# A row softmax on one core: the unrolled stream replaced by hardware loops of three turns over five slots, with placed loop heads and the last tile on its own

## The chip, the cores and the metric

The kernel runs on one core of one Trainium2 chip. The metric is the device time of one execution in microseconds (us), median over several executions.

Engines: DVE is VectorE, ACT is ScalarE, SP is SyncE, which here only issues loads. Sixteen DMA engines move the data.

## The reference

```python
def reference(x, temperature):            # x: (32, 512, 1024) float32, temperature 0.5
    scaled = x / temperature
    shifted = scaled - np.max(scaled, axis=-1, keepdims=True)
    exp_x = np.exp(shifted)
    return (exp_x / np.sum(exp_x, axis=-1, keepdims=True)).astype(np.float32)
```

There are 16,384 rows of 1,024 numbers: 67.11 MB are read and 67.11 MB are written.

## The kernel before

A tile is 1,024 rows: 128 partitions with 8 rows of 4 KiB each, so 32 KiB per partition and 4 MiB per tile. There are 16 tiles and six buffers. SP issues the loads, ACT the stores. A tile is worked on in two groups of four rows. The order is pipelined by one group: the maximum and the exponentials of group g come before the division of group g-1, so a tile's last division waits behind the first maximum of the next tile.

```python
TILES = [[8]] * 16
BUFS = 6
GROUP = 4
# ... (helpers cut)
    def maximum(g):       # DVE: tensor_reduce over 128x4x1024, then bias = -scale * top
    def exponential(g):   # ACT: four activations Exp(scale*x + bias), in place, with accum_out
    def divide(g):        # DVE: reciprocal of the sums, then four in-place multiplies
    def store(g):
        i, _, _, part = groups[g]
        if part:
            a, k = part
            nc.scalar.dma_start(out=dram(of, i)[:, a : a + k, :], in_=tiles[i][:, a : a + k, :])
            if a + k == sum(TILES[i]):
                load()            # the next tile, when its buffer is free

    with tc.manual_schedule():
        for _ in range(BUFS):
            load()
        for g in range(len(groups) + 1):
            if g < len(groups):
                maximum(g)
                exponential(g)
            if g > 0:
                divide(g - 1)
                store(g - 1)
```

Of the kernel before, what the change touches and what calls it, by code (L numbers as in the profile page):

```python
# [1 line left out]

# [4 lines left out]



TILES = [[8]] * 16  # L10
BUFS = 6

GROUP = 4


@with_exitstack
def kernel(
    ctx: ExitStack,
    tc: tile.TileContext,
    x: bass.AP,  # L20
    temperature: bass.AP,
    out: bass.AP,
):
    nc = tc.nc
    f32 = mybir.dt.float32
    scale = 1.0 / float(temperature)
    extreme = mybir.AluOpType.max if scale > 0 else mybir.AluOpType.min

    P = 128
    xf = x.flatten_outer_dims()  # L30
    of = out.flatten_outer_dims()
    n, d = xf.shape
    assert sum(sum(ks) for ks in TILES) * P == n

    data = ctx.enter_context(tc.tile_pool(name="data", bufs=BUFS))
    stats = ctx.enter_context(tc.tile_pool(name="stats", bufs=4))


    groups, first, r = [], [], 0
    for i, ks in enumerate(TILES):  # L40
        first.append(r)
        r += sum(ks)
        a = 0
        for k in ks:
            for b in range(0, k, GROUP):
                m = min(GROUP, k - b)
                groups.append((i, a + b, m, (a, k) if b + m == k else None))
            a += k

    def dram(t, i):  # L50
        k = sum(TILES[i])
        block = t[P * first[i] : P * (first[i] + k), :]
        return block.rearrange("(p k) d -> p k d", p=P, k=k)

    tiles, small = [], []

    def load():
        i = len(tiles)
        if i < len(TILES):
            xt = data.tile([P, sum(TILES[i]), d], f32, name="xt")  # L60
            nc.sync.dma_start(out=xt, in_=dram(xf, i))  # L61
            tiles.append(xt)

    def maximum(g):
        i, a, k, _ = groups[g]
        top, bias, sums, recip = (
            stats.tile([P, k], f32, name=name) for name in ("top", "bias", "sums", "recip")
        )
        small.append((bias, sums, recip))
        nc.vector.tensor_reduce(  # L70
            out=top, in_=tiles[i][:, a : a + k, :], axis=mybir.AxisListType.X, op=extreme
        )
        nc.vector.tensor_scalar_mul(bias, in0=top, scalar1=-scale)  # L73

    def exponential(g):
        i, a, k, _ = groups[g]
        bias, sums, _ = small[g]
        for b in range(k):
            nc.scalar.activation(  # L79
                tiles[i][:, a + b, :],  # L80
                tiles[i][:, a + b, :],
                mybir.ActivationFunctionType.Exp,
                bias=bias[:, b : b + 1],
                scale=scale,
                accum_out=sums[:, b : b + 1],
            )

    def divide(g):
        i, a, k, _ = groups[g]
        _, sums, recip = small[g]  # L90
        nc.vector.reciprocal(recip, sums)  # L91
        for b in range(k):
            nc.vector.tensor_scalar_mul(  # L93
                tiles[i][:, a + b, :], in0=tiles[i][:, a + b, :], scalar1=recip[:, b : b + 1]
            )

    def store(g):
        i, _, _, part = groups[g]
        if part:
            a, k = part  # L100
            nc.scalar.dma_start(out=dram(of, i)[:, a : a + k, :], in_=tiles[i][:, a : a + k, :])
            if a + k == sum(TILES[i]):
                load()



    with tc.manual_schedule():
        for _ in range(BUFS):
            load()
        for g in range(len(groups) + 1):  # L110
            if g < len(groups):
                maximum(g)
                exponential(g)
            if g > 0:
                divide(g - 1)
                store(g - 1)


# [1 line left out]
_INS = ['x', 'temperature']  # L120
_OUTS = [((32, 512, 1024), 'float32')]

_NUMBERS = {'temperature': 0.5}


# [26 lines left out]
```

## Time and profile before

| | before |
|---|---|
| time, median (3 runs at first; 6 runs with the change) | 318.15 us; 318.08 us |
| span of the profiled run | 316.0 us |
| DMA, whole span | 134.25 MB, 425 GB/s |
| DVE busy, ACT busy | 235.5 us (75%), 149.6 us (47%) |
| interval between tiles in the middle (first maximum to first maximum) | 19.35 us |

The page of the kernel before has two rows for the DMA engines over 40 slices of the span (busy tenths, then GB/s), and a part with the queues: q1 are the loads, q10 the stores, q14 the packets that the page calls instruction (below they are read as fetches of instructions).

```profile
DMA  8999999999999999999999999999999999999996
GB/s 332 411 452 423 373 460 415 452 425 431 436 427 440 427 444 423 444 419 448 415 452 411 452 408 456 423 444 427 436 431 432 440 423 444 419 444 419 452 411 274
...
q1 hardware_dynamic: 2304, 67.11, 49.7%
q10 hardware_dynamic: 2304, 67.11, 49.2%
q14 instruction: 4, 0.03, 0.0%
```

The DMA engines are full from start to end. The next view gives stretches of the span of the kernel before; the last two columns are the mean share of the 16 DMA engines that was busy, and GB/s.

```profile
core 0: us, DVE busy (x) ACT busy (x) POOL busy (x), PEclk, DMA share, GB/s
...
100.00:200.00 100.00, 76.31 (x76) 48.84 (x85) 0.00 (x0) 1.00 1.01 435
200.00:280.00 80.00, 59.22 (x57) 39.28 (x68) 0.00 (x0) 1.00 1.00 433
...
310.00:312.00 2.00, 0.00 (x0) 0.00 (x0) 0.00 (x0) 1.00 0.95 410
312.00:314.00 2.00, 0.00 (x0) 0.00 (x0) 0.00 (x0) 1.00 0.42 180
314.00:316.00 2.00, 0.00 (x0) 0.00 (x0) 0.00 (x0) 1.00 0.00 0
```

The middle runs at 433 to 435 GB/s with a busy share of 1.00 to 1.01.

The timeline of DVE in the kernel before, steady part (start, duration, engine, line, operation). In brackets is the idle time before the instruction and what ended it:

```profile
243.90 4.42 DVE L70 TENSOR_REDUCE top<-xt 128x4 f32<-128x4096 f32 x1 [4.88 <-DMA xt<-in_x_dram]
...
251.29 4.41 DVE L70 TENSOR_REDUCE top<-xt 128x4 f32<-128x4096 f32 x1
...
256.02 2.74 DVE L93 TENSOR_SCALAR xt<-xt,recip 128x1024 f32<-128x1024 f32 x4
263.25 4.42 DVE L70 TENSOR_REDUCE top<-xt 128x4 f32<-128x4096 f32 x1 [4.49 <-DMA xt<-in_x_dram]
```

A tile costs DVE about 14.8 us; then it waits 4.5 us for the next load. DVE does not bound the kernel.

### The profile page before, as it was taken

Reading aid. Unit: us, or ns where it says so; the run is one execution under the profiler, and the core shown is the slowest. Engines: PE = TensorE matmul, PEld = TensorE weight load, DVE = VectorE, ACT = ScalarE, POOL = GpSimd, SP = SyncE. Lnnn points to the kernel's source line nnn. Section 1 sums busy time; section 2 is a strip of 40 time slices with the busy share of each in tenths; the row PEclk is TensorE's granted clock in tenths of the full one; section 3 lists DMA queues with packets and bytes.
Section 4 is the critical chain, followed back from the end, with each engine's and each line's share of the span. In section 5 each row is a group of like instructions: output and inputs, shape, how many; then the busy total and the mean of one; then the engine's idle time right before and its main releaser. Section 6 shows DMA issues by size and latency. Waiting matters only on the chain.

```text
span 316.0 us, 620 instructions
## 1 busy us (share of the span) xinstructions
DVE 235.5 (75%) x224; ACT 149.6 (47%) x257; POOL 0.2 (0%) x4
## 2 busy tenths in 40 slices
DVE  0399999999689494994949859497693976949720
ACT  0176666666526255361554605546064560645500
POOL 0000000000000000000000000000000000000000
DMA  8999999999999999999999999999999999999996
GB/s 332 411 452 423 373 460 415 452 425 431 436 427 440 427 444 423 444 419 448 415 452 411 452 408 456 423 444 427 436 431 432 440 423 444 419 444 419 452 411 274
DMA packets 4612, 134.25 MB, mean 425 GB/s; under 512 B 512, under 2 KB 512, under 8 KB 512
## 3 DMA queue, kind: packets, MB, share of 16 engines
q1 hardware_dynamic: 2304, 67.11, 49.7%
q10 hardware_dynamic: 2304, 67.11, 49.2%
q14 instruction: 4, 0.03, 0.0%
HBM read 67.11 MB, written 67.11 MB: 425 GB/s over the span
## 4 chain that ended last, share of the span: by engine, by line
DVE 49%; DMA 32%; another core or an unknown queue 9%; ACT 5%; issue 1%; DVEq 0%; SPq 0%
DVE top L70 29%; DMA xt<-in_x_dram 20%; DVE xt L93 18%; DMA out_dram<-xt 12%; ACT xt L79 5%; DVE recip L91 1%; DVE bias L73 1%; DVEq L147 0%; SPq L61 0%
## 5 line engine op out<-in xcount | busy, mean ns | idle before, releaser
L79 ACT ACTIVATE xt<-xt,bias 128x1024 f32<-128x1024 f32 x128 | 145.4, 1137 | 136.8 <-DVE recip L91 119.4
L70 DVE TENSOR_REDUCE top<-xt 128x4 f32<-128x4096 f32 x32 | 141.3, 4416 | 62.6 <-DMA xt<-in_x_dram 62.6
L93 DVE TENSOR_SCALAR xt<-xt,recip 128x1024 f32<-128x1024 f32 x128 | 87.7, 749 | 1.1
L79 ACT ACTIVATION_READ_ACCUMULATOR xt<-xt,bias 128x1 f32 x128 | 23.9, 187 | 0.0
L79 ACT ACT_TABLE_LOAD x1 | 1.3, 1283 | 13.0 <-DMA xt<-in_x_dram 13.0
L91 DVE RECIPROCAL recip<-sums 128x4 f32<-128x4 f32 x32 | 5.5, 171 | 2.1 <-ACT xt L79 2.1
L73 DVE TENSOR_SCALAR bias<-top 128x4 f32<-128x4 f32 x32 | 5.4, 170 | 1.1
L133 POOL MEMSET const-bfloat16-1.0<- 128x1 bf16 x1 | 0.1, 101 | 0.0
L133 POOL MEMSET const-uint8-127<- 128x1 uint8 x1 | 0.1, 101 | 0.0
L133 POOL MEMSET const-float32-0.0<- 128x1 f32 x1 | 0.1, 98 | 0.2 <-issue 0.2
L133 POOL MEMSET const-float32-1.0<- 128x1 f32 x1 | 0.1, 98 | 0.0
## 6 DMA issues: line engine op xcount, KB each, us to landing
xt<-in_x_dram SPq DMA_DIRECT2D x16, 4096.0 KB, 50.2
out_dram<-xt ACTq DMA_DIRECT2D x16, 4096.0 KB, 38.6
```

What stands on the lines that cost most here:

```text
L70: nc.vector.tensor_reduce(out=top, in_=tiles[i][:, a : a + k, :], axis=mybir.AxisListType.X, op=extreme)
L73: nc.vector.tensor_scalar_mul(bias, in0=top, scalar1=-scale)
L79: nc.scalar.activation(tiles[i][:, a + b, :], tiles[i][:, a + b, :], mybir.ActivationFunctionType.Exp, bias=bias[:, b : b + 1], scale=scal ...
L91: nc.vector.reciprocal(recip, sums)
L93: nc.vector.tensor_scalar_mul(tiles[i][:, a + b, :], in0=tiles[i][:, a + b, :], scalar1=recip[:, b : b + 1])
L133: nc = _bacc.Bacc("TRN2", target_bir_lowering=False, num_devices=1)
```

## The change

The intent is a much shorter program. DVE and ACT run a hardware loop of three turns over five slots of 32 KiB per partition; the sixteenth tile follows the loop and leaves in two halves. Semaphores are handled by hand. Each loop's head is placed by the argument `head_slot` (66); the program has padding ahead of the head and jumps over it. A tile is now finished before the next is begun.

```diff
-TILES = [[8]] * 16
-BUFS = 6
+SLOTS = 5
+ROWS = 8
+LAST = [4, 4]
 GROUP = 4
+HEAD = 66
# ... (most helpers cut)
+    def take(engine, sem, count=1):
+        engine.wait_ge(sem, count).then_inc(sem, -count)
+    def tile_on_vector(s, ends):
+        take(nc.vector, loaded[s], 16)
+        for a in starts:
+            maximum(s, a)
+        for a in starts:
+            divide(s, a, ends)
+    with tc.tile_critical():
+        for t in range(turns):
+            for s in range(SLOTS):
+                if t > 0:
+                    nc.sync.wait_ge(stored[s], 16 * t)
+                nc.sync.dma_start(...).then_inc(loaded[s], 16)
+        nc.sync.wait_ge(stored[0], 16 * turns)
+        nc.sync.dma_start(out=ring[:, 0], in_=last_tile(xf)).then_inc(loaded[0], 16)
+        with nc.vector.bass.Fori(0, turns, engines=[nc.vector.engine], head_slot={nc.vector.engine: HEAD}):
+            for s in range(SLOTS):
+                tile_on_vector(s, [ROWS])
+        tile_on_vector(0, ends)
+        # ... (one warm-up activation)
+        with nc.scalar.bass.Fori(0, turns, engines=[nc.scalar.engine], head_slot={nc.scalar.engine: HEAD}) as t:
+            for s in range(SLOTS):
+                for a in starts:
+                    exponential(s, a)
+                take(nc.scalar, scaled)
+                nc.scalar.dma_start(out=by_turn(of)[s][:, bass.ds(t, 1), :], ...).then_inc(stored[s], 16)
+        for a in starts:
+            exponential(0, a)
+        for k, b, sem in zip(LAST, ends, finished):
+            take(nc.scalar, scaled)
+            nc.scalar.dma_start(out=last_tile(of)[:, b - k : b, :], ...).then_inc(sem, 16)
# ... (final waits cut)
```

More of the change, by code (lines that the diff above doesn't have):

```diff
@@ L32 @@
     n, d = xf.shape
-    assert sum(sum(ks) for ks in TILES) * P == n
-    data = ctx.enter_context(tc.tile_pool(name="data", bufs=BUFS))
-    stats = ctx.enter_context(tc.tile_pool(name="stats", bufs=4))
-    groups, first, r = [], [], 0
-    for i, ks in enumerate(TILES):
-        first.append(r)
-        r += sum(ks)
-        a = 0
-        for k in ks:
-            for b in range(0, k, GROUP):
-                m = min(GROUP, k - b)
-                groups.append((i, a + b, m, (a, k) if b + m == k else None))
-            a += k
@@ L50, in dram @@
-    def dram(t, i):
-        k = sum(TILES[i])
-        block = t[P * first[i] : P * (first[i] + k), :]
-        return block.rearrange("(p k) d -> p k d", p=P, k=k)
-    tiles, small = [], []
-    def load():
-        i = len(tiles)
-        if i < len(TILES):
-            xt = data.tile([P, sum(TILES[i]), d], f32, name="xt")
-            nc.sync.dma_start(out=xt, in_=dram(xf, i))
-            tiles.append(xt)
-    def maximum(g):
-        i, a, k, _ = groups[g]
-        top, bias, sums, recip = (
-            stats.tile([P, k], f32, name=name) for name in ("top", "bias", "sums", "recip")
-        )
-        small.append((bias, sums, recip))
-        nc.vector.tensor_reduce(
-            out=top, in_=tiles[i][:, a : a + k, :], axis=mybir.AxisListType.X, op=extreme
-        )
-        nc.vector.tensor_scalar_mul(bias, in0=top, scalar1=-scale)
@@ L75, in exponential @@
-    def exponential(g):
-        i, a, k, _ = groups[g]
-        bias, sums, _ = small[g]
-        for b in range(k):
-            nc.scalar.activation(
-                tiles[i][:, a + b, :],
-                tiles[i][:, a + b, :],
-                mybir.ActivationFunctionType.Exp,
-                bias=bias[:, b : b + 1],
-                scale=scale,
-                accum_out=sums[:, b : b + 1],
-            )
-    def divide(g):
-        i, a, k, _ = groups[g]
-        _, sums, recip = small[g]
-        nc.vector.reciprocal(recip, sums)
-        for b in range(k):
-            nc.vector.tensor_scalar_mul(
-                tiles[i][:, a + b, :], in0=tiles[i][:, a + b, :], scalar1=recip[:, b : b + 1]
-            )
@@ L97, in store @@
-    def store(g):
-        i, _, _, part = groups[g]
-        if part:
-            a, k = part
-            nc.scalar.dma_start(out=dram(of, i)[:, a : a + k, :], in_=tiles[i][:, a : a + k, :])
-            if a + k == sum(TILES[i]):
-                load()
-    with tc.manual_schedule():
-        for _ in range(BUFS):
-            load()
-        for g in range(len(groups) + 1):
-            if g < len(groups):
-                maximum(g)
-                exponential(g)
-            if g > 0:
-                divide(g - 1)
-                store(g - 1)
+    tiles = n // (P * ROWS)
@@ new lines, with by_turn, last_tile @@
+    turns = tiles // SLOTS
+    assert tiles == turns * SLOTS + 1 and tiles * P * ROWS == n
+    assert sum(LAST) == ROWS and ROWS % GROUP == 0
+    def by_turn(t):
+        whole = t[: turns * SLOTS * ROWS * P, :]
+        return whole.rearrange("(t s p k) d -> s p t (k d)", s=SLOTS, p=P, k=ROWS)
+    def last_tile(t):
+        return t[turns * SLOTS * ROWS * P :, :].rearrange("(p k) d -> p k d", p=P, k=ROWS)
+    pool = ctx.enter_context(tc.tile_pool(name="data", bufs=1))
+    ring = pool.tile([P, SLOTS, ROWS, d], f32, name="ring")
@@ new lines @@
+    top = pool.tile([P, ROWS], f32, name="top")
+    bias = pool.tile([P, ROWS], f32, name="bias")
+    sums = pool.tile([P, ROWS], f32, name="sums")
+    recip = pool.tile([P, ROWS], f32, name="recip")
+    warm = pool.tile([P, 1], f32, name="warm")
+    loaded = [tc.alloc_semaphore(f"loaded{s}") for s in range(SLOTS)]
+    stored = [tc.alloc_semaphore(f"stored{s}") for s in range(SLOTS)]
+    finished = [tc.alloc_semaphore(f"finished{j}") for j in range(len(LAST))]
+    topped, biased, summed, inverted, scaled = (
+        tc.alloc_semaphore(name)
+        for name in ("topped", "biased", "summed", "inverted", "scaled")
+    )
@@ new lines, in take, with maximum @@
+    def take(engine, sem, count=1):
+        engine.wait_ge(sem, count).then_inc(sem, -count)
+    starts = range(0, ROWS, GROUP)
+    def maximum(s, a):
+        nc.vector.tensor_reduce(
+            out=top[:, a : a + GROUP],
+            in_=ring[:, s, a : a + GROUP, :],
+            axis=mybir.AxisListType.X,
+            op=extreme,
+        ).then_inc(topped, 1)
+        take(nc.vector, topped)
+        nc.vector.tensor_scalar_mul(
+            bias[:, a : a + GROUP], in0=top[:, a : a + GROUP], scalar1=-scale
+        ).then_inc(biased, 1)
@@ new lines, in exponential, with divide @@
+    def exponential(s, a):
+        take(nc.scalar, biased)
+        for r in range(a, a + GROUP):
+            ins = nc.scalar.activation(
+                ring[:, s, r, :],
+                ring[:, s, r, :],
+                mybir.ActivationFunctionType.Exp,
+                bias=bias[:, r : r + 1],
+                scale=scale,
+                accum_out=sums[:, r : r + 1],
+            )
+        ins.then_inc(summed, 1)
+    def divide(s, a, ends):
+        take(nc.vector, summed)
+        nc.vector.reciprocal(recip[:, a : a + GROUP], sums[:, a : a + GROUP]).then_inc(
+            inverted, 1
+        )
+        take(nc.vector, inverted)
+        for r in range(a, a + GROUP):
+            ins = nc.vector.tensor_scalar_mul(
+                ring[:, s, r, :], in0=ring[:, s, r, :], scalar1=recip[:, r : r + 1]
+            )
+            if r + 1 in ends:
+                ins.then_inc(scaled, 1)
@@ new lines, in tile_on_vector @@
+    def tile_on_vector(s, ends):
[4 more added lines that the diff above has]
+            divide(s, a, ends)
+    ends = [sum(LAST[: j + 1]) for j in range(len(LAST))]
+    with tc.tile_critical():
[3 more added lines that the diff above has]
+                    nc.sync.wait_ge(stored[s], 16 * t)
+                nc.sync.dma_start(
+                    out=ring[:, s].rearrange("p k d -> p (k d)"), in_=by_turn(xf)[s][:, t, :]
+                ).then_inc(loaded[s], 16)
+        nc.sync.wait_ge(stored[0], 16 * turns)
[4 more added lines that the diff above has]
+        tile_on_vector(0, ends)
+        nc.scalar.activation(
+            warm, nc.const_aps.tensor(0.0, (P, 1)), mybir.ActivationFunctionType.Exp
+        )
+        with nc.scalar.bass.Fori(0, turns, engines=[nc.scalar.engine], head_slot={nc.scalar.engine: HEAD}) as t:
[3 more added lines that the diff above has]
+                take(nc.scalar, scaled)
+                nc.scalar.dma_start(
+                    out=by_turn(of)[s][:, bass.ds(t, 1), :],
+                    in_=ring[:, s].rearrange("p k d -> p (k d)").unsqueeze(1),
+                ).then_inc(stored[s], 16)
+        for a in starts:
+            exponential(0, a)
+        for k, b, sem in zip(LAST, ends, finished):
+            take(nc.scalar, scaled)
+            nc.scalar.dma_start(
+                out=last_tile(of)[:, b - k : b, :], in_=ring[:, 0, b - k : b, :]
+            ).then_inc(sem, 16)
+        for s in range(SLOTS):
+            nc.sync.wait_ge(stored[s], 16 * turns)
+        for sem in finished[:-1]:
+            nc.sync.wait_ge(sem, 16)
@@ L120 @@
+    with tc.tile_critical():
+        nc.sync.wait_ge(
+            finished[-1], 16, synchronizes=[nc.sync.lower_ap(ring[:, 0, ROWS - 1, :])]
+        )
 _INS = ['x', 'temperature']
```

## The prediction

> **What bounds the kernel now.** The DMA engines. The page's DMA row is 9 in every slice but the first and the last; 134.25 MB move in a span of 316.0 us. In the table of stretches the DMA engines carry 435 GB/s from 100 to 200 us and 433 GB/s from 200 to 280 us, with a busy share of 1.00 to 1.01.[...] Reading and writing 67.11 MB each at 434 GB/s takes 309 us (estimate). The rest is about 1 us before data flows, some 2 us lost to 422 GB/s while only loads run, and about 2.8 us after the last byte (the stretch 313 to 314 us carries 66 GB/s, the next 0). DVE is busy 235.5 us (75%), ACT 149.6 us (47%); neither is at its limit.
>
> **What changes.** Bytes, transfers and row length (32 KiB) stay. The compute instructions stay in number and shape. Removed: one slot of six, the interleaving in which a tile's last divide waits behind the next tile's first maximum, and the unrolled streams. Added: separate semaphore instructions, loop back edges (two per engine), and one more store because the last tile leaves in halves.
>
> **The new DVE chain.** DVE now finishes a tile before it begins the next. From the first tile of the timeline: two reductions and two biases 9.2 us; the eight exponentials end 13.83 us after the tile's start; reciprocal and four multiplies then take 2.95 us, so 16.8 us. Five or so exposed semaphore instructions[...] give about 17.4 us per tile, against 14.8 us of DVE work now. DMA needs 19.3 us per tile (8.39 MB at 434 GB/s). So DVE stays below DMA, with about 1.9 us to spare per tile[...].[...]
>
> **Five slots.** A slot's cycle is 5 x 19.3 = 97 us: 17.4 us of compute, about 80 us in the two DMA queues, so some four tiles are queued at any time. DMA doesn't run dry. Stores leave about 17.5 us after landing, no longer 27 us, which gives back most of what the sixth slot held.
>
> **The tail.** The last load lands near 282 us. Its halves are ready about 12.4 and 17.4 us later. The backlog of stores then is about 1.7 tiles, some 17 us at full rate (estimate), so DMA stays full and the split has no gap to fill. The ending stays at about 313 us of data plus 3 us.
>
> **Prediction.** 317.6 us, with a range of 315.8 to 320.0 us; faster by over 2%: 0.02, within 2%: 0.92, slower by over 2%: 0.06.
>
> **What would show it right.** DMA row again 9 throughout, 430 to 435 GB/s in the middle; maxima of steady tiles still wait 1 to 2 us for their load; gap between a tile's first maximum and its last multiply about 17.4 us; last data near 313 us.
>
> **What would make it wrong.** If a DVE tile costs over about 18 us with its share of the back edge, DVE becomes the limit and each extra 0.3 us per tile adds nearly 5 us: the maxima would then no longer wait for loads and DMA slices would fall under 9.[...] A costlier start or finish would shift everything by up to 1 us.

The DVE sum came to 17.4 us per tile: 16.8 us from the trace, and the estimate for the exposed semaphore instructions. The some 2 us lost while only loads run are the author's estimate; from 1 to 33 us the trace has 423 GB/s. Of the last paragraph, the 18 us and the 1 us were estimates.

## The result, and the profile after

The changed kernel takes 320.63 us (median of 6 runs, 320.31 to 321.21), against 318.08 us before (317.94 to 318.2). The ratio is 1.0082, 95% interval 1.0069 to 1.0095. A ratio is the mean time of one kernel's fast runs over that of the other's of the same rounds, so it is not quite the ratio of the medians. The change costs 2.55 us.

The same part of the page for the changed kernel:

```profile
DMA  8999999999999999999999999999999999999992
GB/s 323 403 451 431 390 431 447 406 449 431 427 451 402 451 427 431 455 398 455 423 435 447 406 455 423 435 447 406 447 431 435 447 406 447 431 427 455 406 421 121
...
q1 hardware_dynamic: 2304, 67.11, 49.1%
q10 hardware_dynamic: 2448, 67.11, 48.7%
q14 instruction: 6, 0.05, 0.1%
```

The middle is as full as it was. The last slice fell from 274 to 121 GB/s, and q14 has six packets for four. (q10 has 144 packets more because the last tile leaves in two halves.) The stretches of the changed kernel:

```profile
core 0: us, DVE busy (x) ACT busy (x) POOL busy (x), PEclk, DMA share, GB/s
...
100.00:200.00 100.00, 84.17 (x76) 50.81 (x87) 0.00 (x0) 1.00 1.01 435
200.00:280.00 80.00, 61.41 (x61) 39.25 (x69) 0.00 (x0) 1.00 1.00 432
...
312.00:314.00 2.00, 0.00 (x0) 0.00 (x0) 0.00 (x0) 1.00 0.71 303
314.00:316.00 2.00, 0.00 (x0) 0.00 (x0) 0.00 (x0) 1.00 0.08 33
316.00:318.00 2.00, 0.00 (x0) 0.00 (x0) 0.00 (x0) 1.00 0.04 16
```

This is the loss. After 314 us the mean share is 0.08 and then 0.04. With 16 engines, 0.06 is one engine. So after 314 us almost all the engines are done, and one DMA engine writes the rest of the output: the landing times below show it alone for the last 3.3 us (the last but one lands at 314.89 us, the last at 318.16 us).

DVE of the changed kernel, steady part:

```profile
229.60 4.42 DVE L74 TENSOR_REDUCE top<-ring 128x4 f32<-128x4096 f32 x1 [2.12 <-DVEq L69]
...
234.24 4.41 DVE L74 TENSOR_REDUCE top<-ring 128x4 f32<-128x4096 f32 x1
...
239.57 2.74 DVE L105 TENSOR_SCALAR ring<-ring,recip 128x1024 f32<-128x1024 f32 x4 [0.15 <-DVEq L69]
...
244.21 2.74 DVE L105 TENSOR_SCALAR ring<-ring,recip 128x1024 f32<-128x1024 f32 x4
249.06 4.42 DVE L74 TENSOR_REDUCE top<-ring 128x4 f32<-128x4096 f32 x1 [2.11 <-DVEq L69]
```

From 229.60 to the end of the last multiply at 246.95 a tile takes 17.35 us; then DVE waits 2.1 us for the load. ("DVEq L69" is the separate wait instruction.) DVE is still not the limit.

### Reading single DMA engines

The views average over the 16 DMA engines, but the trace has a record of every packet: start, duration, queue, size. A data packet is one partition's 32,768 B here and lasts 1.21 us. On one engine a packet starts within some 10 ns of the end of the packet before (3 to 4 ns before it at the median). So each record can be hung behind the record that it follows, and the 16 engines come apart. (Where two engines' packets end within a few ns of each other, this can swap them; sums over all engines don't depend on it.) And each transfer has 16 landings (512 for the 32 transfers before, 528 for 33 in the changed kernel), one by each engine, so they show directly how far the last engine is behind.

The last store (of the changed kernel: its second half) in the two profiled runs, in us:

| | before | changed |
|---|---|---|
| median engine lands | 313.63 | 313.89 |
| last engine lands | 315.18 | 318.16 |
| **lag of the last engine** | **1.55** | **4.27** |
| from there to the end of the run | 2.68 | 3.05 |
| time of this run | 317.86 | 321.21 |

The difference of 3.35 us between these two runs is 0.26 (the median engine; the first load is issued at 0.94 us for 0.73) + 2.72 (the lag) + 0.37 (the ending). So 2.72 of 3.35 us is a single DMA engine that came late.

Where does it lose its time? The packets of that engine and of a typical one in the changed kernel follow. L is a load packet, S a store packet, I an instruction packet, an asterisk is the end of a transfer (its semaphore write), the number after @ is the start; a duration in parentheses is given where it is above 1.24 us.

```
last engine, changed:  I@2.1 L@3.3 L@4.5 L@5.8 L@7.0 I@8.2 L@8.5(1.82) L@10.3 ...
                       S@66.1 I@67.3 L@67.6(1.75) S@69.4 ...
                       S@91.3 L*@92.5 S@92.5(1.36) L@93.8 S*@95.1 L@95.1(1.34) S@96.4 ...
typical, changed:      L@2.2(1.92) L@4.1 L@5.4 L@6.6 L@7.8 L@9.0 ...
                       L*@87.1 S@87.1 L@88.3 S@89.6 L@90.8 S@92.0 L@93.2 S*@94.4 L@94.4 S@95.6 ...
```

Two things are to be seen. First, this engine carried three of the six instruction packets: the first took 1.25 us, the others 0.31 us each, and the data packet after these two took 1.82 and 1.75 us where 1.21 is normal; so these two put the engine back by 0.92 and 0.85 us. (The packets are 8,192 B each. In the kernel before the four took 0.31 us each and the data packets after them 1.48 to 1.75 us; two of them were on the engine that was 1.55 us behind at the end.) Second, near the ends of transfers some of its packets are slow by 0.1 us, again and again, tile after tile; the typical engine has none of these. On the typical engine a load ends six packets before a store (L\*@87.1, S\*@94.4); on the last engine it ends two packets before (L\*@92.5, S\*@95.1). Below this number is called the distance.

Loads and stores take turns packet by packet, with one 32 KiB record per turn: in the changed kernel, from 60 to 280 us, all 2,542 data packets whose predecessor on the engine is unambiguous follow a packet of the other queue. What one engine loses stays with it: in the traces a lag shrank by 0.3 us at most between two losses. Counted packet by packet, the last engine of the changed kernel was 1.4 us behind the median engine after its two early instruction packets, 2.0 us at 58 us, 2.8 us after the third instruction packet at 67.3 us, and 4.3 us at the end. The last 1.5 us are the small losses at the ends of transfers.

### The profile page after: what moved, and what is told of

It is laid out like the page before. It is cut to its first block, busy times and chain, and to the rows that moved or that the text cites. A ratio compares the mean times of both kernels' runs of the same rounds, so it can differ in the third digit from the quotient of the medians.

```text
span 319.4 us, 789 instructions
## 1 busy us (share of the span) xinstructions
DVE 237.9 (74%) x224; ACT 149.8 (47%) x258; POOL 0.2 (0%) x4
## 5 line engine op out<-in xcount | busy, mean ns | idle before, releaser
L88 ACT ACTIVATE ring<-ring,bias 128x1024 f32<-128x1024 f32 x128 | 145.4, 1136 | 151.4 <-ACTq L69 151.3
L74 DVE TENSOR_REDUCE top<-ring 128x4 f32<-128x4096 f32 x32 | 141.2, 4414 | 28.5 <-DVEq L69 28.5
L105 DVE TENSOR_SCALAR ring<-ring,recip 128x1024 f32<-128x1024 f32 x128 | 87.7, 747 | 4.8 <-DVEq L69 1.2
L88 ACT ACTIVATION_READ_ACCUMULATOR ring<-ring,bias 128x1 f32 x128 | 23.9, 186 | 0.0
```

What stands on the lines that cost most here:

```text
L74: nc.vector.tensor_reduce(out=top[:, a : a + GROUP], in_=ring[:, s, a : a + GROUP, :], axis=mybir.AxisListType.X, op=extreme,).then_inc(to ...
L88: ins = nc.scalar.activation(ring[:, s, r, :], ring[:, s, r, :], mybir.ActivationFunctionType.Exp, bias=bias[:, r : r + 1], scale=scale, a ...
L105: ins = nc.vector.tensor_scalar_mul(ring[:, s, r, :], in0=ring[:, s, r, :], scalar1=recip[:, r : r + 1])
```

## The experiments

Four theories were on the table after the first look. F: instruction fetches run on the very DMA engines that bound the kernel, and they make one engine late. S: the missing sixth slot. D: the longer serial chain on DVE. E: the ending in halves. After the first runs a fifth was added, P, and then sharpened to P2: where the first store falls between the packets of the running load decides the distance on each engine, and a bad distance costs time in every tile.

In every table, "before" is the kernel before in the same rounds. The lag is that of the last store in the profiled run of the kernel.

### a1, a2: without the head placement; without the loops

```diff
# a1
-Fori(0, turns, engines=[...], head_slot={...: HEAD})
+Fori(0, turns, engines=[...])
# a2
-with nc.vector.bass.Fori(...):      (and the same for ACT)
+for t in range(turns):
```

> The changed kernel without the placement of the loop heads; all else stays. Theory F (one DMA engine carries the instruction fetches, falls behind the other fifteen and ends the kernel alone): the four 8 KiB instruction packets that the changed kernel has between 1.9 and 8.5 us go away, the last store's slowest engine comes under 2.5 us after the median engine (4.27 us in the changed kernel, 1.55 us before), and the time falls to about 318.3 us, ratio to before 0.999 to 1.003. Rival S (five slots) and rival D (serial DVE chain) and rival E (the ending in halves) all leave it at about 320.6 us, ratio 1.007 to 1.009.[...]

> The changed kernel with both hardware loops written out three times; slots, semaphores, order and ending stay. Theory F: no packets at the start, but later ones as the longer streams run on; each costs its DMA engine some 0.85 us of lag; with two packets on an engine as before, 318 to 319 us, ratio 1.000 to 1.004. Rivals S, D and E: unchanged at 320.6 us, ratio about 1.008.

| | time, median (all) | before | ratio | instruction packets | lag |
|---|---|---|---|---|---|
| a1 | 319.91 (319.63 to 323.71) | 318.02 | 1.010 [1.0058, 1.0142] | 2, none before 9 us | 3.01 |
| a2 | 321.90 (319.65 to 324.31), and one of 324.80 | 318.02 | 1.0159 [1.0122, 1.0196] | 6, none before 9 us | 2.74 |

(The 324.80 counts as slow because it is over 1.5% above the fastest run of a2; its clock was 1.000. The ratio of a2 can be reproduced only with this run kept in; the five fast runs alone give 1.0127. And the profiled runs of a1 and a2, 319.72 and 319.65 us, are among the fastest, so their traces don't show the worst of the scatter.) The four early packets went away with the head placement, as F expected, but the time did not go to 318.3, and the runs now scatter by 4 to 5 us. a2 missed the 318 to 319 us of F as well. F alone is not enough. The loops are not the cause either, since the scatter is there without them. In a2 there were slow packets, away from instruction packets, of 4.19 us in all between 60 and 280 us, in a1 2.70 us, in the changed kernel 1.67 us, and in the kernel before 0.00 us.

### a3: five buffers in the kernel before

```diff
-BUFS = 6
+BUFS = 5
```

> The kernel before with five buffers for six, nothing else. Rival S: the fifth slot is what costs, so 320.5 us, ratio 1.007 to 1.009. Theory F: within 0.1% of before, 318.1 us, with the same instruction packets.

It took 317.96 us (317.75 to 318.24), ratio 0.9999 [0.9986, 1.0012], lag 1.77 us. S falls: the sixth buffer was worth nothing.

### a4: an empty placed loop ahead of the kernel before

```diff
+    with tc.tile_critical():
+        for eng in (nc.vector, nc.scalar):
+            with eng.bass.Fori(0, 1, engines=[eng.engine], head_slot={eng.engine: 66}):
+                pass
     with tc.manual_schedule():
```

> The kernel before with one empty one-turn loop on the vector and on the scalar engine ahead of everything, its head placed at slot 66: adds the jump over the padding and the fetches after it, none of the slots, order or ending. Theory F: instruction packets appear in the first 10 us, the slowest engine's lag at the last store grows from 1.55 us by 1 to 2.7 us and the time by the same, to 319 to 321 us. Rivals S, D and E: 318.1 us.

It took 330.31 us, ratio 1.0392 [1.0378, 1.0405], but it failed as an experiment. The added block held up the second load: from 12 to 18 us the DMA engines moved 82 GB/s. It did leave something behind. The first store came at a different place, all engines stood at distance 2 or 3, and 262 slow packets cost 70 us summed over the 16 engines. That pointed to the distance.

### b1, b2: the first store later, with and without loops

A dummy multiply on DVE after the first load delays all stores. It does no useful work.

```diff
+        nc.vector.wait_ge(loaded[0], 16)
+        nc.vector.tensor_scalar_mul(
+            scratch, in0=ring[:, 0].rearrange("p k d -> p (k d)")[:, :DELAY], scalar1=1.0
+        )
         (the loop on DVE follows; b1: a2 with DELAY = 3200; b2: a1 with DELAY = 2980)
```

> The written-out changed kernel with one dummy multiply of about 1.8 us on the vector engine after the first load, so that every store is issued 1.8 us later (the first at about 32.6 us as in the kernel before, not 30.8 us). Theory P (what matters is where the first store falls between the packets of the running load: where it arrives near a packet's end, some DMA engines take a store packet before a load packet and others after, and an engine out of step then loses about 0.1 us per tile and ends alone): all 16 engines take their first store packet within one packet time, the lag of the last engine stops growing apart from instruction packets, 318.2 to 319.0 us, spread of the runs under 0.7 us (5.2 us without the delay). Rivals (serial DVE chain, own semaphores, ending in halves): unchanged or 1.8 us slower, 319.7 to 325 us.

> The changed kernel with loops but no head placement, and the same dummy multiply, about 1.7 us, so that the first store is issued at about 32.65 us and not 30.97 us. Theory P: one step on all engines, two instruction packets only, so a last-store lag of 0.5 to 1.5 us where it was 3.0, 318.0 to 318.8 us, small spread (4.1 us without the delay). Rivals: 319.6 to 324 us.

| | first store issued | time, median (all) | ratio | instruction packets | distance | lag |
|---|---|---|---|---|---|---|
| a2 | 30.80 us | 321.90 (319.65 to 324.31), slow: 324.80 | 1.0159 | 6 | 2 and 4 | 2.74 |
| b1 | 32.55 us | 319.33 (319.07 to 319.62) | 1.0039 [1.0027, 1.0051] | 6 | 6 on all | 2.42 |
| a1 | 30.97 us | 319.91 (319.63 to 323.71) | 1.010 | 2 | 2 and 4 | 3.01 |
| b2 | 32.29 us | 317.69 (317.62 to 317.91) | 0.9989 [0.9976, 1.0002] | 2 | 6 on all | 0.71 |

Adding a useless multiply of 1.83 and 1.71 us to DVE made the two kernels 2.6 and 2.2 us faster (medians of fast runs, in different rounds) and took the scatter away. D falls with this: b2 has the serial chain, the five slots, the hand-made semaphores, the loops and the ending in halves, and it is level with the kernel before (its 317.69 us lie 0.3 us below the range expected for it). The stretches of b2 show the ending:

```profile
312.00:314.00 2.00, 0.00 (x0) 0.00 (x0) 0.00 (x0) 1.00 0.65 279
314.00:316.00 2.00, 0.00 (x0) 0.00 (x0) 0.00 (x0) 1.00 0.00 0
```

No engine works alone after 314 us. b1 missed its expected range by 0.3 us: its distance is good, but it has six instruction packets, and its lag grew where they came: 0.5 us before the first pair at 63 and 68 us, about 1 after, and 1.7 us by 244 us.

### b3, b4, c2, c3: delays of the kernel before, looking for a bad place

```diff
# a3, and ahead of the first maximum:
+        nc.vector.tensor_scalar_mul(
+            scratch, in0=tiles[0].rearrange("p k d -> p (k d)")[:, :DELAY], scalar1=1.0
+        )
         (b3: DELAY = 1420, b4: 2072, c2: 500, c3: 1000)
```

> The kernel before with five buffers (318.0 us) and a dummy multiply of about 0.87 us ahead of the first maximum, so that the first store is issued at about 33.5 us, not 32.6, and arrives where the engines' packets end (about 37.1 to 37.6 us). Theory P: some engines out of step, lag grows during the run to 2.5 us or more, 319 to 322 us with a spread over 1 us. Theory that only instruction packets make the lag, and all rivals: 318.0 to 318.3 us, since the DMA engines have work throughout.

> As b3 but with a delay of about 1.21 us, one packet time, so that the first store falls between packet ends again. Theory P: like the kernel before, 318.0 to 318.4 us with a small spread; if a later store simply costs more, it is slower than b3.

> The kernel before with five buffers and a dummy multiply of about 0.3 us, first store issued at about 32.9 us. It lies between 32.6 us (in step, 318.0 us) and 33.5 us (in step one packet later, 317.6 us). Theory P: if the store arrives while packets end, some engines start at 37.2 and others at 38.4 us, and then the time is 318.8 us or more, with a spread over 1 us. If all start together, 317.6 to 318.1 us and the point is missed again.

> As the one before with about 0.55 us, first store issued at about 33.15 us. Theory P: engines split between 37.2 and 38.4 us, 318.8 us or more; if all start together, 317.6 to 318.1 us.

| | first store issued | first store packet on the 16 engines | time, median (all) | ratio |
|---|---|---|---|---|
| a3 | 32.60 us | 37.1 to 37.6 | 317.96 (317.75 to 318.24) | 0.9999 |
| c2 | 33.03 us | 5 at 37.0 to 37.3, 11 at 38.4 to 38.9 | 317.81 (317.65 to 318.13) | 1.0000 [0.9987, 1.0013] |
| c3 | 33.18 us | 2 at 37.1 to 37.3, 14 at 38.3 to 38.6 | 317.96 (317.63 to 318.62) | 1.0002 [0.9989, 1.0015] |
| b3 | 33.50 us | 38.4 to 38.9 | 317.59 (317.5 to 318.19) | 0.9987 [0.9975, 1.0000] |
| b4 | 33.65 us | 38.3 to 38.7 | 317.73 (317.68 to 317.9) | 0.9989 [0.9976, 1.0002] |

b3 was expected to be slow and was not: its delay jumped over the packet ends. b4 came in 0.3 us below its range. c2 and c3 did split the engines into two groups, and still nothing was lost. So P in its first form is wrong: being out of step with the other engines costs nothing. What these runs have in common is that nearly every load ends six or eight packets from a store, a few four, and none two.

Sorted by distance, all 18 traces together (transfers that end between 60 and 280 us; the loss is the sum over slow packets directly around the two ends, those just after instruction packets left out):

```
load ends ... packets before the store     2      3      4      6      8
cases (one engine, one tile)             281     23    610   1283    371
mean loss, us                          0.158  0.629  0.011  0.000  0.000
cases with any loss                      64%    65%     5%     1%     0%
```

This is P2. (The table holds d1 and d2 as well, so it is a summary; the test of P2 is d1 and d2 themselves, below.) Two and three are best read together (304 cases, 0.19 us): a second count from the same records put nearly all of these cases at two, with the same sum, so that three packets look worse than two is not shown. Counted with up to three packets around the ends, the mean is 0.31 us at two or three (301 cases), 0.02 us at four, and still 0.000 us at six and eight. Most of the cases at two come from a4 and d1 (below), where most engines stood badly; in the changed kernel there are 11, all on one engine and all with loss. Where the store ended four to eight packets before the load (605 cases) the mean loss was 0.005 us. Other combinations are rare: distances 1 and 5 have 15 cases, and in 15 more the store ended two packets before the load or together with it, without loss.

### c1, d3: the changed kernel with its first store later

```diff
# c1: the dummy multiply ahead of the loop, DELAY = 700
# d3: inside the loop, at the first slot of each turn
         take(nc.vector, loaded[s], 16)
+        if s == 0:               (so also for the sixteenth tile)
+            nc.vector.tensor_scalar_mul(
+                scratch, in0=ring[:, 0].rearrange("p k d -> p (k d)")[:, :DELAY], scalar1=1.0
+            )
```

> The changed kernel as it is, heads placed at slot 66, with a dummy multiply of about 0.4 us after the first load, so that the first store is issued at about 32.5 us and not 32.1. Theory P with packets: the six instruction packets stay (four of them before 9 us), the other engines now take their first store packet in one step; the last-store lag falls from 4.27 us to between 1.2 and 3 us, 318.2 to 319.8 us. If the head placement does all of it by its packets alone, the lag stays above 4 us and the time at 320.6 us. The comparison with the same delay without the head placement (317.7 us) then gives what the placement costs.

> The changed kernel with its placed heads and a dummy multiply of about 0.4 us inside the loop (at slot 0 of each turn), so that nothing new stands ahead of the loop. First store at about 32.5 us. P2: all engines at distance 4 or 6, no growth between tiles; what is left is the instruction packets, six of them: last-store lag 1.8 to 3 us, 318.6 to 319.6 us. Against 317.7 us without placement that is the price of the placement. If distance does not matter: 320.6 us.

c1 took 319.89 us (319.42 to 321.12), ratio 1.0065 [1.005, 1.0079], but its first store was issued at 38.0 us, not at 32.5. (The lag of its last store was 1.18 us, but only because the median engine was late as well: it landed at 315.78 us.) The timeline of DVE in c1 shows why:

```profile
13.89 0.53 DVE L135 TENSOR_SCALAR scratch<-ring 128x700 f32<-128x700 f32 x1 [13.89 <-DMA ring<-in_x_dram]
20.40 4.42 DVE L77 TENSOR_REDUCE top<-ring 128x4 f32<-128x4096 f32 x1 [5.99 <-DVEq L72]
```

The tile was loaded, yet DVE stood still for 5.99 us. Instruction packets ran at 18.43 and 24.15 us. In the changed kernel four instruction packets come before 9 us, while DVE waits for the first load anyway. With the wait now ahead of the loop, the jump to the placed head comes after the load and not at the start. That DVE waited here for a fetch that the full DMA had delayed is inference from these times; the trace does not show it. So c1 did not test what it should; d3 did.

d3 took 319.72 us (319.09 to 320.29), ratio 1.0056 [1.0042, 1.0069]. All engines stood at distance 4 or 6. The lag of its loads was 3.48 us at 71.70 us and 3.37 us at 284.60 us: it no longer grew. The last-store lag was 2.10 us, within the expected 1.8 to 3 us, but the time is 0.1 us above the range. The last engine of d3 has its three instruction packets nearly where the changed kernel has them; counted as above, it was 1.2 us behind after the first two, 1.3 us at 58 us, 2.1 us after the third and 2.1 us at the end. So the instruction packets cost what they cost before, and the 1.5 us of small losses are gone. With about the same good distance, the price of the placed heads is then the difference between d3 and b2: ratios 1.0056 and 0.9989, so 0.67% or 2.1 us (they ran in different rounds; the lags of the profiled runs, 2.10 and 0.71 us, differ by 1.4 us, and the profiled run of d3 is its fastest).

### c4, d4: the sixteenth tile in one part

```diff
-LAST = [4, 4]
+LAST = [8]          (in b2: c4; d4 also has DELAY = 5400)
```

> The version with loops, no head placement and the late first store (317.69 us), but the sixteenth tile stored in one part. If the DMA engines have a backlog of stores when the last tile is ready, the split is worth nothing: 317.6 to 317.9 us. If the split fills a gap, 0.5 us or more slower.

> Loops without placement, sixteenth tile in one part, first store about 2.7 us later than without delay (issued at about 33.5 us, distance 8 or 6). P2: 317.4 to 317.8 us with a spread under 0.5 us, as the version with 1.5 us; the best of the versions so far or level with it.

c4: 317.67 us (317.64 to 318.71), ratio 0.9993 [0.998, 1.0006]. d4: 317.84 us (317.82 to 318.22), ratio 0.9994 [0.9981, 1.0008], first store issued at 33.71 us, lag 0.93 us. E falls: in one part or in two the ending is the same, because the DMA engines have stores left (in the changed kernel the last half is issued at 305.5 us, and the DMA share from 302 to 310 us is 0.99). d4 was not better than b2, only as good; it fell just outside its expected 317.4 to 317.8.

### d1, d2: distance 2 made and unmade in the kernel before

This is the test of P2. The kernel before, six buffers, gets dummy in-place multiplies on the first tile: eleven, about six packet times, or fourteen and a half, meant as eight packet times. A turn of loads and stores has sixteen packets, so the first should give distance 2 and the second distance 6 again. (Measured, the first store moved by 7.2 us, six packet times, in d1, but by 8.7 us, a little over seven, in d2. Neither put all engines at one distance, as the table shows.)

```diff
+        for b in range(DUMMIES):                 (d1: 11; d2: 14 and one of half a row)
+            row = tiles[0][:, b % 8, :]
+            nc.vector.tensor_scalar_mul(row, in0=row, scalar1=1.0)
         for g in range(len(groups) + 1):
```

> The kernel before, six buffers, with eleven dummy in-place multiplies ahead of the first maximum: the first store is issued about 7.3 us later, six packet times, so that every engine ends each load two packets before it ends a store (distance 2; before it is 6). Theory P2 (a DMA engine loses about 0.16 us in each tile at distance 2, and nothing at 4, 6 or 8): slow packets on most engines, 319.6 us or more with a spread over 1 us. Theory that only instruction packets count, and theory that an engine merely out of step with the others loses: 317.6 to 318.3 us.

> As d1 with about 9.7 us, eight packet times, so distance 6 again though the store is later still. Theory P2: 317.6 to 318.3 us, no slow packets away from the instruction packets. If a late start of the stores is what costs, it is slower than d1.

| | first store issued | distance | slow packets 60 to 280 us, sum over 16 engines | time, median (all) | ratio |
|---|---|---|---|---|---|
| before | 32.66 us | 6 (a few 8) | 0.00 us | 318.25 (317.86 to 318.56) | |
| d1 | 39.87 us | 2 (71 cases), 4 (98) | 33.7 us in 167 | 322.25 (320.79 to 323.21) | 1.0139 [1.0121, 1.0156] |
| d2 | 41.39 us | 4 (76), 6 (69), 2 or 3 (14) | 0.59 us in 3 | 317.88 (317.67 to 317.9) | 0.999 [0.9976, 1.0003] |

The time and the spread of d1, and the time of d2, came out as P2 expected; the distances did so only on part of the engines. One engine of d1, in the notation of above:

```
d1:  S@78.9 L*@80.1 S@80.1 L@81.4 S*@82.6 L@82.6(1.60) S@84.2 L@85.4(1.60) S@87.0
```

A store that is issued 7.2 us later costs 4 us, and one that is issued 8.7 us later costs nothing. It is not lateness, and not the program's structure: the kernel before, with its own order, buffers and ending, loses time and scatters as soon as loads end two packets before stores on many of its engines. The stretches of d1 near the end, and then those of d2:

```profile
312.00:314.00 2.00, 0.00 (x0) 0.00 (x0) 0.00 (x0) 1.00 1.10 475
314.00:316.00 2.00, 0.00 (x0) 0.00 (x0) 0.00 (x0) 1.00 0.46 197
316.00:318.00 2.00, 0.00 (x0) 0.00 (x0) 0.00 (x0) 1.00 0.19 82
...
312.00:314.00 2.00, 0.00 (x0) 0.00 (x0) 0.00 (x0) 1.00 0.50 213
314.00:316.00 2.00, 0.00 (x0) 0.00 (x0) 0.00 (x0) 1.00 0.00 0
```

Several engines of d1 are late, not one. Its cases at distance 4 lost something too (4.9 us in 107 cases between 45 and 280 us), and in d2 the 14 cases at 2 or 3 lost nothing. The distance decides the odds, not every case; whether engines at two also slow down their neighbours at four was not tested.

## Why the prediction was wrong

The prediction was 317.6 us, 315.8 to 320.0 us; 320.63 us was measured. That it stayed within 2% was right. Step by step:

- **DMA bounds the kernel, and its middle stays full.** Right: 435 and 432 GB/s against 435 and 433.
- **The DVE chain takes about 17.4 us per tile and stays below DMA.** Right: the first tile takes 17.27 us from its first maximum to the next one's (14.55 to 31.82 us), the steady tile 17.35 us. The maxima wait 2.1 us for their loads, about the 1 to 2 us that were expected. A back edge shows no cost on DVE: the last multiplies of a turn end at 100.93 us, and the first maximum of the next turn starts at 100.85 us, the same small overlap as inside a turn.
- **Five slots are enough.** Right, shown by a3.
- **The split of the last tile has no gap to fill.** Right, shown by c4.
- **"The ending stays at about 313 us of data plus 3 us."** This is the step that failed. The median DMA engine did land its last bytes at 313.89 us, but one engine landed at 318.16 us. The prediction treated 16 engines as one pipe with one rate. The term of the sum that was mis-sized is the lag of the last engine: taken as unchanged (1.55 us), it was 4.27 us in the profiled run (which is the slowest of the six). The same lag shows in the last load: it was expected near 282 us, the median engine landed it at 281.21 us, and the last engine at 287.88 us.
- **What the fetches do to DMA was missing.** No back edge made DVE wait (above), but the prediction did not ask whether instruction fetches take time from the DMA engines. In the changed kernel four instruction packets came in the first 9 us (at 1.92, 2.07, 6.61 and 8.18 us), after the branches ahead of the placed heads; a1, without the placement, has none there. No compute engine is seen to stand still for want of instructions (the trace puts the idle time of DVE and ACT, 59.1 and 151.3 us, down to waits for semaphores); the DMA engines were held up. (The first load was one of the things held up: its last engine landed at 14.42 us in the changed kernel and at 13.23 us in a1, which has no placed heads.) With a good distance they are worth about 2 us (d3 against b2).
- **That the first store's moment matters was missing altogether.** Earlier stores (32.14 us for 32.66 us, and one engine already late from its fetches) put one engine at distance 2. Its slow packets cost 1.6 us in the trace. In the medians, removing it gained 0.9 us (320.63 to 319.72 us, the changed kernel to d3, in different rounds). That is a small step: the intervals of the two ratios, [1.0069, 1.0095] and [1.0042, 1.0069], just touch. The surer evidence is packet by packet, and d1.

So two causes make up the 2.55 us: the placed heads with their early fetches, about 2 us, and the small losses on one engine, about 0.9 us. (Together that is a little more, since b2, which has neither, is a little faster than the kernel before.)

What stays open: why a DMA engine loses time when its load ends two or three packets before its store. The traces show when it happens and how much it costs, not what the engine does then. c1 also had slow packets on many engines at 66 to 68 and 74 to 79 us, at distances that were good elsewhere; with 17.9 us in 34 packets between 60 and 280 us they are no small matter, and they are not explained. So the distance is not the only thing that makes packets slow. The 0.37 us by which the stretch from the last landing to the end of the run is longer was not looked into; it belongs to the new program, not to the late engine (3.02 to 3.05 us in all versions of the changed kernel, 2.59 to 2.80 us in all versions of the kernel before), and b2 is level in spite of it.

A version that is clearly better than both kernels was not found. b2 (0.9989 [0.9976, 1.0002]) and b3 (0.9987 [0.9975, 1.0000]) are level with the kernel before or a little better, and b2 (317.69 us) is some 2.9 us faster than the changed kernel (320.63 us), though in different rounds.

## What to carry to other kernels

When DMA is the bound, look at the landing times of the single DMA engines at the end and not only at the mean rate: here the kernel ended with its slowest engine (318.16 us, the median engine at 313.89 us), and what that engine lost early was still missing at the end (1.4 us behind after its first two instruction packets, 4.3 us at the end). The lag at the last store went from 0.09 us (a4, where nearly all engines were slowed alike) to 4.27 us (the changed kernel). Instruction fetches, of which there were six with placed loop heads and two without (a1), used the same DMA engines here, so in this DMA-bound kernel they had a price (about 2 us) even where no compute engine was seen to wait for them. If a kernel that streams in and out scatters by a per cent or slows after a harmless edit, it is a cheap test to shift the first store by a packet time or two: here that took up to 2.6 us away (b1), and a shift by six packet times added 4 us (d1).
